# The sum of three weight quarters in the Mixer: two accumulating loads in place of an addition on VectorE, under a new list of instructions

## The chip, the cores and the metric

The kernel runs on one core of a Trainium2 chip. A core has five engines that run their own instruction streams: TensorE (PE in the profile, with its weight loads as PEld), VectorE (DVE), ScalarE (ACT), GpSimd (POOL) and SyncE (SP), and 16 DMA engines that serve the queues on which the engines put transfers. The metric is the device time in microseconds, and less is better. The kernel is launched once, and the weights lie in HBM in the layout that the kernel wants.

## The reference

One decoder layer on 512 tokens with 1,024 features, in float32:

```python
h = h + 0.5 * swiglu(rmsnorm(h, ffn1_norm), ffn1_w_gate, ffn1_w_up, ffn1_w_down)   # 1024 -> 2816 -> 1024
n = rmsnorm(h, mix_norm)
u, v, z, xbc, dt_raw = jnp.split(n @ w_in, IN_SPLITS, axis=-1)                     # u, v, z: 1024 columns each
ya = rmsnorm(chunked_spatial_gating(gelu(u), gelu(v), ...), gm_out_norm)
yb = mamba2_mixer(z, xbc, dt_raw, ...)                                             # conv, chunked SSD, silu(z), norm
h = h + jnp.concatenate([ya, yb], axis=-1) @ w_out
h = h + 0.5 * swiglu(rmsnorm(h, ffn2_norm), ffn2_w_gate, ffn2_w_up, ffn2_w_down)
gate = jax.nn.sigmoid(rmsnorm(h, ple_norm) @ ple_w_gate + ple_b_gate)
h = h + gate * (p @ ple_w_proj)
return rmsnorm(h, final_norm)
```

What matters here are the three products `n @ w_u`, `n @ w_v` and `n @ w_z` of the token mixer, each 512 x 1024 by 1024 x 1024.

## The kernel before, in words

**Precision.** Every float32 operand of a large product is split into a high part, the fp32r copy, and a low part, the rest. A product is three TensorE passes: high by high, high by low and low by high. For a weight tile of 128 x 1024 the split is a ScalarE copy into `whi` and a VectorE subtraction into `wlo` (`Parts.split`); the tile itself comes by one 512 KB load on SP's queue (`Parts.load`).

**Seven products.** The weights w_u, w_v and w_z are each cut into two blocks of 512 columns, and each block into four quarters of 512 rows by 256 columns: `src[0]`, `src[1]` are the upper and lower rows of the first 256 columns, `src[2]`, `src[3]` those of the second. A block is computed not by eight products of quarters but by seven products of sums of quarters, in the manner of Strassen and Winograd. The sums of the activations are made once. Those of the weights are made block by block, in `Quads.run`, most of them by the transfer itself: a load on GpSimd's queue with `accum_op=ALU.add` adds the quarter in HBM to the tile in SBUF. One product is 24 matmuls with 256 columns.

A block uses three tiles of weights: `w11` and `w22`, which live through most of the block and are changed and split again in between (pool `r4`, two buffers, shown as `r` in the profile), and `w`, which is used for one product (pool `raw`, three buffers). In the order of the program text: `w11` is loaded with `src[0]` and split for product 1; `w` gets `src[2] + src[0]` for product 7; `w22` is loaded with `src[3]`, split for later use, and `src[2]` is added to it by an accumulating load for the sum of products 5 and 6; product 4 uses its split of `src[3]`. Then VectorE adds `w22` to `w11`, so that `w11` is `src[0] + src[2] + src[3]`; that is split for product 6. `src[1]` is added to `w11` by an accumulating load, for product 3. Product 5 uses `w22`, product 2 a fresh `w` with `src[1]`. There are six such blocks: two each in `gates` (w_z), `values` (w_v, where weights and activations change sides on TensorE) and `outer` (w_u), called z0, z1, v0, v1, u0, u1 here.

**The order.** The program is not issued as it is written. Each call on an engine is recorded (`Recorder`), the records are grouped into units (a unit is one instruction, or a row of TensorE instructions with the same output), numbered from 0 in the order of the program text, and issued in the order of a list, `ORDER` (line 87), by `issue` under a manual schedule. There are 2,729 units. Each engine, and each queue of transfers, gets its instructions in the order of that list and runs them in that order; a semaphore wait is put in wherever an operand isn't ready or a buffer isn't free. Buffers are handed out in the order of the list too: a tile takes the first buffer that is free in its pool at its first use, and gives it back after its last. All instructions have line 1906 in the profile, since `issue` makes the call, so that they are told apart by the names of their tiles: `r` is w11 or w22, `raw` the tile `w`, `whi` and `wlo` the split, `xa` and `xb` the activations in the blocks of the Mixer, `xfa` and `xfb` in the SwiGLU stages, `m` and `u` the tiles of the SSD, `b` and `a` the accumulators in PSUM.

**Stages.** By the names of the tiles in the trace, the first SwiGLU runs to about 356 us, the Mixer's convolution part, SSD, blocks and `w_out` follow, the six blocks between 425 and 585 us interleaved with the SSD and the gating, then the second SwiGLU from about 680 us, the gated embedding, and the final norm (`factors`, `rows_out`) from about 1059 us: 32 transposes of 128 x 128 (`ident`), and sums of squares by matmuls with `ones`.

Of the kernel before, what the change touches and what calls it, by code (L numbers as in the profile page):

```python
# [27 lines left out]
ALU = mybir.AluOpType  # L28
# [48 lines left out]
for _name, _w in _VECS:  # L77
# [212 lines left out]
def layer_kernel(ctx: ExitStack, tc: tile.TileContext, a: dict, out: bass.AP):  # L290
# [1139 lines left out]
    class Quads:  # L1430
# [23 lines left out]
        def run(self, plain, summed):  # L1454
            src = self.src
            w11 = Parts("r4")
            w11.load(src[0])
            w11.split()
            ps_x, ps_a, ps_q = bank(), seeded(), bank()
            self.product(w11, 1, ps_x, True)  # L1460
            nc.scalar.copy(ps_a, ps_x)
# [552 lines left out]
```

## Time and profile before

| | |
|---|---|
| runs of the kernel before | 1073.25, 1074.03, 1074.38 us; median 1074.03 |
| the profiled execution | 1075.2 us |
| its span, first to last instruction | 1073.5 us |
| mean granted TensorE clock | 0.996 |
| data moved by DMA | 173.28 MB |

The profile is of one execution. Its own time is 1.7 us above its span, and 1.2 us above the median of the runs. Engine rows give busy time, share of the span and number of instructions. A row of a group names line, engine, operation, output `<-` inputs, shape and count, then the summed time with the mean in ns, then the idle time of that engine just before these instructions, with what ended most of it. A row of DMA issues gives the count, the KB of each and the median time from issue to landing. A row that begins with a time is an event, or a few in a row that are alike: start, duration, engine, what it did, `x` the count. A row of a stretch begins with its bounds, then its length and the busy time and number of instructions of PE, PEld, DVE, ACT and POOL, the granted clock, the mean busy share of the 16 DMA engines and GB/s. In the rows of the waits, the numbers are the idle time in us, how often, and the longest.

### The profile page before, as it was taken

The page shows a single profiled execution, that of the slowest core. Times are in us where ns is not written, and L with a number is a line of the kernel's source. Part 1 is how long each engine was busy: PE and PEld are TensorE (multiplying, and loading weights), DVE is VectorE, ACT ScalarE, POOL GpSimd, SP SyncE. Part 2 cuts the span into 40 slices and gives each one's busy share as a digit, 9 for nine tenths or more (in the row PEclk, how much of TensorE's full clock was granted, in tenths as well). Part 3 has the DMA queues.
Part 4 walks back from the last instruction along what each step waited for, and adds up shares of the span by engine and source line. Part 5 has one row for each costly group of instructions (what it writes and reads, how often), then busy time and mean ns, then how long its engine had stood idle before and what let it go on. Part 6 is the DMA issues. An engine that isn't in the chain of part 4 may idle for free.

```text
span 1073.5 us, 17640 instructions
## 1 busy us (share of the span) xinstructions
PE 1065.4 (99%) x7151; PEld 967.5 (90%) x7151; DVE 816.0 (76%) x1169; ACT 560.3 (52%) x781; POOL 77.1 (7%) x95
## 2 busy tenths in 40 slices
PE   9999999999999999999999999999999999999997
PEld 7899999999998878998999888999999999999887
DVE  6888676756577879999999667888766666757765
ACT  7555343444444537897766344655344343434544
POOL 1100000110100000000100000010100100000000
PEclk9999999999999999999999999999999999999998
DMA  9967775575633244776765444767936855734312
GB/s 322 250 169 204 202 191 197 146 209 137 177 79 99 62 135 131 182 216 164 204 144 127 135 136 106 213 187 198 261 98 197 232 142 145 186 121 112 112 53 79
DMA packets 52210, 173.28 MB, mean 161 GB/s; under 512 B 5920, under 2 KB 6176, under 8 KB 52128
## 3 DMA queue, kind: packets, MB, share of 16 engines
q1 hardware_dynamic: 34272, 117.98, 32.0%
q0 software_dynamic: 12256, 44.57, 23.1%
q10 hardware_dynamic: 5600, 9.60, 3.0%
q8 instruction: 56, 0.92, 0.3%
q14 instruction: 26, 0.21, 0.1%
HBM read 167.86 MB, written 4.26 MB: 160 GB/s over the span
## 4 chain that ended last, share of the span: by engine, by line
PE 99%; DMA 0%; ACT 0%; SPq 0%; DVE 0%; issue 0%; ACTq 0%
PE b L1906 81%; PE a L1906 18%; DMA g<-in_p 0%; SPq L1906 0%; DVE glo L1906 0%; ACT o L1906 0%; ACT ghi L1906 0%; ACT m L1906 0%; ACT b L1906 0%; ACTq L1906 0%
## 5 line engine op out<-in xcount | busy, mean ns | idle before, releaser
L1906 PE MATMUL b<-xfb,whi 128*128 128x256 f32 (+1 forms) x1704 | 298.1, 279 | 0.7 <-ACT b L1906 0.7
L1906 PEld LDWEIGHTS b<-xfb,whi 128*128 128x128 f32 x1704 | 260.8, 188 | 6.5 <-issue 1.0
L1906 PE MATMUL b<-xfb,wlo 128*128 128x256 f32 (+1 forms) x852 | 237.2, 278 | 0.0
L1906 ACT CAST whi<-raw 128x1024 fp32r<-128x1024 f32 (+1 forms) x131 | 136.4, 1042 | 148.5 <-PE b L1906 82.6
L1906 DVE TENSOR_TENSOR wlo<-raw,whi 128x1024 fp32r<-128x1024 f32 (+1 forms) x130 | 157.2, 1213 | 54.0 <-ACT whi L1906 51.4
L1906 PEld LDWEIGHTS b<-xfb,wlo 128*128 128x128 f32 x852 | 159.9, 188 | 0.5
L1906 PE MATMUL b<-xfa,whi 128*128 128x256 f32 (+1 forms) x696 | 124.2, 281 | 0.0
L1906 PEld LDWEIGHTS b<-xfa,whi 128*128 128x128 f32 x696 | 107.0, 188 | 2.9 <-DVE xfa L1906 0.5
L1906 PE MATMUL b<-xfa,wlo 128*128 128x256 f32 (+1 forms) x348 | 97.8, 281 | 0.0
L1906 ACT CAST whi<-rawb 128x1024 fp32r<-128x1024 f32 x51 | 53.5, 1050 | 67.1 <-PE b L1906 54.2
L1906 DVE TENSOR_TENSOR wlo<-rawb,whi 128x1024 fp32r<-128x1024 f32 x51 | 62.3, 1221 | 25.0 <-ACT whi L1906 25.0
L1906 ACT CAST whix<-rawd 128x1024 fp32r<-128x1024 f32 (+1 forms) x40 | 39.4, 986 | 76.0 <-PE a L1906 41.5
L1906 DVE TENSOR_TENSOR wlox<-rawd,whix 128x1024 fp32r<-128x1024 f32 (+1 forms) x40 | 45.7, 1142 | 34.0 <-ACT whix L1906 33.9
L1906 PE MATMUL b<-m,whi 128*128 128x512 f32 x224 | 69.5, 391 | 0.0
L1906 PEld LDWEIGHTS b<-xfa,wlo 128*128 128x128 f32 x348 | 65.4, 188 | 0.5
L1906 PE MATMUL b<-xb,whi 128*128 128x256 f32 (+1 forms) x280 | 61.9, 317 | 0.0
L1906 PE MATMUL b<-ghi,wlox 128*128 128x512 f32 x156 | 61.4, 394 | 0.0
L1906 PE MATMUL b<-glo,whix 128*128 128x512 f32 x156 | 61.2, 392 | 0.0
L1906 PE MATMUL b<-ghi,whix 128*128 128x512 f32 x156 | 60.7, 389 | 0.0
L1906 POOL DMA_DIRECT2D raw<-in_ffn_gu x32 | 31.7, 1034 | 344.2 <-DVE wlo L1906 126.3
L1906 PE MATMUL a<-ghi,wlox 128*128 128x512 f32 x140 | 55.2, 394 | 0.0
L1906 PE MATMUL a<-glo,whix 128*128 128x512 f32 x140 | 54.9, 392 | 0.0
(294 smaller groups left out, 2256.9 us busy)
## 6 DMA issues: line engine op xcount, KB each, us to landing
raw<-in_ffn_gu SPq DMA_DIRECT2D x57, 512.0 KB, 6.2
rawd<-in_ffn_down SPq DMA_DIRECT2D x40, 512.0 KB, 4.5
raw<-in_ffn_gu POOLq DMA_DIRECT2D x32, 512.0 KB, 7.6
rawb<-in_ffn_gu SPq DMA_DIRECT2D x31, 512.0 KB, 6.1
s<-in_ffn_gu SPq DMA_DIRECT2D x21, 512.0 KB, 4.9
s<-in_ffn_gu POOLq DMA_DIRECT2D x21, 512.0 KB, 7.9
raw<-in_w_out SPq DMA_DIRECT2D x16, 512.0 KB, 3.7
raw<-in_w_in SPq DMA_DIRECT2D x13, 512.0 KB, 3.8
```

The costliest lines, as they stand in the source:

```text
L1906: getattr(getattr(real, engine), what)(*(real_of(x) for x in args), **{k: real_of(x) for k, x in kw.items()})
```

## The change

In each of the six blocks the addition on VectorE goes. In its place `w11` gets two accumulating loads on GpSimd's queue: `src[2]` after the first split of `w11`, and `src[3]` later; each is 512 KB. Nothing that the block computes is different but for the order of that sum. `ORDER` is a new list for the whole program. With six instructions fewer and twelve more it has 2,735 units, and their numbers shift accordingly.

```diff
@@ -85,130 +85,130 @@
 ORDER = (
-    "1-2 5-7 9-10 13 12 11 0 3 14 16 18 24 20 15 17 19 25 21 26 41 27 29 42 38 37 40 39 43 8 34 32-33 35 "
...
@@ -1456,6 +1456,7 @@
             w11 = Parts("r4")
             w11.load(src[0])
             w11.split()
+            nc.gpsimd.dma_start(w11.raw, src[2], accum_op=ALU.add)
             ps_x, ps_a, ps_q = bank(), seeded(), bank()
             self.product(w11, 1, ps_x, True)
             nc.scalar.copy(ps_a, ps_x)
@@ -1463,6 +1464,7 @@
             w = Parts()
             w.load(src[2])
             nc.gpsimd.dma_start(w.raw, src[0], accum_op=ALU.add)
+            nc.gpsimd.dma_start(w11.raw, src[3], accum_op=ALU.add)
             w22 = Parts("r4")
             w22.load(src[3])
             w.split()
@@ -1474,7 +1476,6 @@
             nc.gpsimd.dma_start(w22.raw, src[2], accum_op=ALU.add)
             self.product(w22, 4, ps_q, False)
 
-            nc.vector.tensor_tensor(w11.raw, w11.raw, w22.raw, ALU.add)
             w11.split()
             nc.gpsimd.dma_start(w11.raw, src[1], accum_op=ALU.add)
             self.product(w11, 6, ps_a, False)
```

All lines of the list differ; it is left out here but for its first line before. What of it bears on the blocks: on GpSimd's queue, the new list has w11's load of `src[2]`, w11's of `src[3]` and then w22's of `src[2]` in the blocks z0, v0 and u1, and w22's load between w11's two in z1, v1 and u0; ScalarE makes w22's second split ahead of w11's in z0, z1 and u0. TensorE's instructions are the same by name and count, and 1,881 of 6,964 stand elsewhere in the order. In the final norm, four transposes stood ahead of the second half's sums of squares; in the new list all 32 stand behind them.

247 rows, old and new, of the table ORDER are left out of this document.

## The prediction

> **What bounds the kernel now.** I read the page first, then the waits of TensorE alone, then the Mixer stage (425 to 585 us) by windows.
>
> ```profile
> span 1073.5 us, 17640 instructions
> PE 1065.4 (99%) x7151; PEld 967.5 (90%) x7151; DVE 816.0 (76%) x1169; ACT 560.3 (52%) x781; POOL 77.1 (7%) x95
> ...
> DVE  6888676756577879999999667888766666757765
> ...
> q0 software_dynamic: 12256, 44.57, 23.1%
> ...
> PE 99%; DMA 0%; ACT 0%; SPq 0%; DVE 0%; issue 0%; ACTq 0%
> ```
>
> ```profile
> PE b L1906 <- DVE tmp L1906: 1.7, 1, 1.7
> PE b L1906 <- ACT b L1906: 0.7, 1, 0.7
> PE a L1906 <- ACT m L1906: 0.3, 1, 0.3
> ```
>
> ```profile
> core 0: us, PE busy (x) PEld busy (x) DVE busy (x) ACT busy (x) POOL busy (x), PEclk, DMA share, GB/s
> 425.00:585.00 160.00, 159.74 (x1334) 151.85 (x1333) 153.76 (x257) 126.12 (x217) 16.23 (x19) 1.00 0.70 175
> ```
>
> The chain that ended last is TensorE for 99% of the span. TensorE waits for another engine three times, 2.7 us in all; 1.7 of that is the wait for the first operand at the start, where the edit reaches nothing. In the Mixer, where the edit lies, TensorE is busy 159.74 of 160 us and VectorE 153.76, which is 96% (the nines of its row on the page). So VectorE is nearly full there, but it is not waited for: the 0.3 us is an ACT copy. Work taken from VectorE gives time back only where TensorE stood still for it, and these rows show no such place.
>
> The addition and its neighbours, in the first of the six blocks:
>
> ```profile
> 440.56 1.05 ACT L1906 CAST whi<-r 128x1024 fp32r<-128x1024 f32 x1 [0.75 <-DMA r<-in_w_z]
> 440.70 1.22 DVE L1906 TENSOR_TENSOR r<-r,r 128x1024 f32<-128x1024 f32 x1
> 442.34 1.05 ACT L1906 CAST whi<-r 128x1024 fp32r<-128x1024 f32 x1
> 443.42 1.23 DVE L1906 TENSOR_TENSOR wlo<-r,whi 128x1024 fp32r<-128x1024 f32 x1
> 444.94 0.80 PE L1906 MATMUL a<-xb,whi 128*128 128x256 f32 x2
> ```
>
> The addition starts when the load onto w22 has landed, the sum is split, and product 6 starts 0.3 us after the split's end at 444.65. The list in force is just in time there: TensorE had other work up to that moment.
>
> **What goes.** Six additions on VectorE:
>
> ```profile
> L1906 DVE TENSOR_TENSOR r<-r,r 128x1024 f32<-128x1024 f32 x6 | 7.3, 1224 | 0.7 <-DMA r<-in_w_u 0.7
> L1906 DVE TENSOR_TENSOR wlo<-r,whi 128x1024 fp32r<-128x1024 f32 x30 | 36.6, 1222 | 2.8 <-ACT whi L1906 2.7
> L1906 ACT CAST whi<-r 128x1024 fp32r<-128x1024 f32 x30 | 31.4, 1047 | 20.3 <-PE b L1906 7.7 <-DVE r L1906 3.6 <-PE a L1906 2.7
> ```
>
> 7.3 us of VectorE, all beside a busy TensorE: I take 0 for it. The bounds are 0 and the waits that TensorE has after the start, 0.7 + 0.3 = 1.0 us gained. Product 6 also no longer depends on w22's data, though in the new list ScalarE still has w22's second split ahead of w11's in three of the blocks (z0, z1, u0).
>
> **What comes.** Twelve accumulating loads of 512 KB on POOL's queue, two to a block. Their nearest rows are the accumulating loads that are there:
>
> ```profile
> q0 software_dynamic: 2448, 8.91, 33.3%
> ...
> r<-in_w_z POOLq DMA_DIRECT2D x4, 512.0 KB, 5.8
> ...
> r<-in_w_z SPq DMA_DIRECT2D x3, 512.0 KB, 3.7
> ...
> raw<-in_w_v POOLq DMA_DIRECT2D x2, 512.0 KB, 9.0
> raw<-in_w_u POOLq DMA_DIRECT2D x2, 512.0 KB, 7.7
> ```
>
> ```profile
> L1906 POOL DMA_DIRECT2D r<-in_w_z x4: 872/874/875, 434.5 to 474.1; - x4
> ```
>
> Issuing costs POOL 0.87 us each, 10 us on a queue that is busy 16 of 160 us: nothing on TensorE's path. The data: q0's 8.91 MB in this stage are 17 loads and take 33.3% of the 16 DMA engines, so 1.96 points each; twelve more are 23.5 points, and the stage's DMA share goes from 0.70 to about 0.94. The second load adds onto what the first wrote, so it waits in POOL's queue until that has landed. By the new list, what stands directly behind it is w22's own accumulating load in the blocks z0, v0 and u1; in z1, v1 and u0 w22's load goes between the two. Behind w22's load waits its second split, and behind that, on ScalarE, in z0 the split for product 6.
>
> The length of the new chain is the cost to look at. From the end of w11's first split to the finished sum are two landings, 2 x 5.8 = 11.6 us. Before, the addition could follow as soon as w22 had landed, 2.4 us after that split in the fourth block (520.38 to 522.76):
>
> ```profile
> 519.16 1.22 DVE L1906 TENSOR_TENSOR wlo<-r,whi 128x1024 fp32r<-128x1024 f32 x1
> ...
> 522.76 1.22 DVE L1906 TENSOR_TENSOR r<-r,r 128x1024 f32<-128x1024 f32 x1
> ```
>
> Such a block has to load w11 some 9 us earlier than it did. There are two r4 buffers, so the question is whether the pair turns over in time. With 2.27 us for a split (1.05 + 1.22), w11 holds its buffer for 3.7 + 2.27 + 11.6 + 2.27 + 5.8 + 2.27 = 27.9 us and w22 for 3.7 + 2.27 + 5.8 + 2.27 = 14.0. Two buffers make that 21.0 us to a block, against (23.3 + 14.0) / 2 = 18.7 before, where w11 has 3.7 + 2.27 + 5.8 for w22's landing, 1.22 for the addition, then 2.27 + 5.8 + 2.27. A block lasts 160 / 6 = 26.7 us. The margin shrinks from 8.0 to 5.7 us and stays above zero, so I take 0; the upper bound is in the rivals. Three landings a block (six for two buffers) use up 5.7 us when each becomes 1.9 us longer.
>
> One rule speaks against moving work from VectorE to these loads. POOL's issue took 872 to 875 ns four times out of four, in a stage where VectorE is busy 96%. The Trainium skill, "SBUF — State Buffer", section "SBUF: two separate sides", says that while VectorE holds the port pair which it shares with GpSimd, GpSimd cannot write the descriptors of its DMAs, and the load looks stalled. By that rule each of a block's two new loads could wait out one 1.22 us operation and the margin of 5.7 would be some 4.5; by the row nothing is held up. I go by the row.
>
> **The list.** It holds the same TensorE instructions before and after (I compared them by name), in another order, so TensorE's sum can change only through its pace. That is not constant:
>
> ```profile
> 509.00:516.00 7.00, 7.00 (x62) 7.00 (x61) 5.84 (x9) 6.17 (x8) 0.00 (x0) 1.00 0.87 300
> ...
> 519.00:526.00 7.00, 7.00 (x64) 7.00 (x64) 6.50 (x10) 5.97 (x12) 0.00 (x0) 1.00 0.99 219
> ```
>
> ```profile
> 507.51 0.94 PE L1906 MATMUL b<-m,m 128*128 128x128 f32 x6
> 508.20 0.36 PE L1906 MATMUL a<-whi,xa 128*128 128x256 f32 x1
> ...
> 517.23 1.20 PE L1906 MATMUL b<-u,m 128*64 128x128 f32 x13
> 518.37 0.38 PE L1906 MATMUL b<-whi,xb 128*128 128x256 f32 x1
> ```
>
> ```profile
> 48.50:61.00 12.50, 12.50 (x112) 12.50 (x112) 11.34 (x15) 10.31 (x14) 0.16 (x1) 1.00 0.51 116
> 707.50:720.00 12.50, 12.50 (x108) 12.50 (x107) 11.19 (x14) 8.36 (x10) 0.00 (x0) 1.00 0.41 100
> ```
>
> The four windows hold only matmuls of 256 columns at full clock, and TensorE never stops; still one pace is 12.5 us / 110.5 = 113.1 ns and the other 12.5 / 106.5 = 117.4 (1.5 taken off each count for the edges). A run keeps the pace with which it starts, until a matmul of another kind comes. The six blocks have 6 x 7 x 24 = 1,008 such matmuls; if about half are slow now (an estimate from the windows above, one each), all slow costs 2.2 us more and all fast 2.2 us less. The slow stretch at 509 follows the SSD matmuls `b<-m,m`, the fast one at 519 follows `b<-u,m`; the new list puts its longest Mixer run, 144 matmuls, behind those. I take -0.5, a little over a hundred matmuls at 4.3 ns.
>
> At the end the list moves four transposes. Now they stand ahead of the second half's sums; in the new list all 32 come after them.
>
> ```profile
> 1059.33 0.63 PE L1906 MATMUL b<-ident,h 128*128 128x128 f32 x4
> ...
> 1059.80 0.50 PE L1906 MATMUL b<-ones,ssum 128*128 128x1 f32 x4
> 1060.17 2.08 PE L1906 MATMUL b<-ones,sq 128*128 128x1 f32 x12
> ...
> 1062.11 5.97 PE L1906 MATMUL b<-ident,h 128*128 128x128 f32 x28
> ```
>
> 28 take 5.97 us, 0.213 each, so four more cost 0.85 at most; the sums start 0.47 earlier (1059.33 instead of 1059.80), and ScalarE scales the last half tile two operations earlier. Between 0 and +0.85 I take +0.3.
>
> **The sum**, on the profiled execution's own 1075.2 us (span 1073.5 and 1.7 around it): 0 for the additions, 0 for the loads, -0.5 and +0.3 for the list, so 1075.0. That execution is 1.2 above the median of the runs, 1074.03: forecast **1073.8**, its own range 1072 to 1076. A difference below 0.2%, 2.1 us, is about what can't be told from no change.
>
> **The rivals.**
>
> *Slower: the loads don't keep up.* Place: w11's buffer in the Mixer. For it: the share of 0.94, and rows in the same stage where an accumulating load takes 7.7 and 9.0 us instead of 5.8; the list is just in time (0.3 us above), so a late sum stops TensorE at once. Against: TensorE lost nothing at a share of 0.99 around 519. It decides from 1.9 us a landing. At 2.6 (between 7.7 and 9.0) a block loses 3 x (2.6 - 1.9) = 2.1 us; in the three blocks where w22's load is queued behind the second, that is 6 us with little given back: 1079 to 1080, less if only one or two blocks slip, 1076 to 1078. The Trainium skill, "DMA: Bandwidth & Descriptors", section "Rules for kernel authors", demands that wait for the earlier load's semaphore, so it can't be queued away.
>
> *Faster: the relief is used.* With 7.3 us free on VectorE, the new order could run all blocks at the quick pace and lose the waits of 0.7 and 0.3: -2.2 - 1.0 = -3.2, so 1070.8. For it: VectorE was full. Against: TensorE, the bound, has nothing left to give but pace, which the free time does not set.
>
> *The search undoes it.* The whole list is new, the two SwiGLU stages too, where nothing of the program changed. One product that comes late by one transfer in each of them, like the wait behind ACT of 0.7, and a slow pace in the blocks (2.2) make +3: 1077. For it: nothing but the number of moved instructions.
>
> **How the numbers follow.** Forecast 0.50, slower 0.20, faster 0.20, the undoing search 0.10. Faster by over 0.2%: the faster rival and a little of the forecast's edge, 0.23. Slower: the two others less what stays within the bound, 0.27. Within: 0.50. The range 1071.2 to 1078.8 leaves out the deep end of each side rival.
>
> **What would show it.** Right: VectorE 7 us lower, q0 at about 50.9 MB instead of 44.6, POOL with twelve more issues, TensorE's waits in the Mixer still near zero, its busy time within 2 us. Wrong: ACT or PE rows waiting for `DMA r<-in_w_*` in the Mixer and TensorE idle before `a<-xb,whi` (slower); TensorE's 1,008 matmuls quicker by 2 us (faster); idle time in the SwiGLU stages (the search).

## The result, and the profile after

The changed kernel takes 1080.71 us (median of four, 1079.80 to 1082.08) against 1073.64 of the kernel before; the ratio is 1.0069, 95% interval 1.0051 to 1.0086. It is slower, by less than 1% but clear of the noise. Two later series beside the kernel before, on two chips, gave 1.0040 (1.0027 to 1.0054) and 1.0044 (1.0030 to 1.0058).

The page of the kernel after:

```profile
span 1078.0 us, 17649 instructions
PE 1065.6 (99%) x7151; PEld 967.5 (90%) x7151; DVE 813.0 (75%) x1163; ACT 560.3 (52%) x782; POOL 85.5 (8%) x107
...
q0 software_dynamic: 13984, 50.86, 26.1%
...
PE 95%; DMA 2%; ACT 1%; DVE 1%; issue 0%; SPq 0%; ACTq 0%
```

The edit is there as it was read: six VectorE instructions fewer, twelve more on POOL, and q0 moves 50.86 MB instead of 44.57. TensorE is as busy as before (1065.4). New is the last line: 5% of the chain is no longer TensorE, where it was 1%. The waits of TensorE in the kernel after:

```profile
PE b L1907 <- DVE tmp L1907: 2.2, 2, 1.7
PE b L1907 <- ACT a L1907: 1.8, 1, 1.8
PE b L1907 <- ACT b L1907: 0.7, 1, 0.7
PE a L1907 <- DVE wlo L1907: 0.6, 2, 0.3
PE b L1907 <- DVE wlo L1907: 0.6, 1, 0.6
PE a L1907 <- ACT m L1907: 0.3, 1, 0.3
PE b L1907 <- DVE glo L1907: 0.2, 1, 0.2
```

The old ones (1.7, 0.7, 0.3) are all there still. Of the new ones, 0.2 us is near the start, at 7.9 us; the other five lie between the first matmul of the blocks and the first of the second SwiGLU. That stretch before, and then after:

```profile
430.24:676.05 245.81, 245.55 (x1719) 222.99 (x1718) 214.03 (x350) 159.86 (x261) 18.00 (x21) 1.00 0.61 158
```

```profile
430.27:681.53 251.26, 247.46 (x1720) 224.40 (x1719) 210.47 (x346) 159.23 (x260) 26.12 (x31) 1.00 0.70 171
```

It is 5.45 us longer: TensorE stands still 3.80 us of it instead of 0.26, and is busy 1.91 us longer for the same matmuls. Up to 430 us the two traces agree within 0.03 us; the second SwiGLU and the embedding take 381.6 and 381.7 us. The final norm takes 15.85 us before (from 1057.63) and 14.81 after (from 1063.23), which is the clock's doing, see the last section. 0.03 + 5.45 + 0.12 - 1.04 is the 4.56 us between the spans.

The stop of 1.8 us is in the first block, z0. By time, in the kernel after:

```profile
427.60 0.85 POOL L1907 DMA_DIRECT2D r<-in_w_z  x1 [5.10 <-DMA r<-in_w_z]
...
428.31 0.33 SPq L1907 DMA_DIRECT2D raw<-in_w_z  x1
...
437.61 1.04 ACT L1907 CAST whi<-raw 128x1024 fp32r<-128x1024 f32 x1 [3.16 <-DMA raw<-in_w_z]
...
439.28 0.57 ACT L1907 COPY a<-b 128x512 f32<-128x512 f32 x1
...
439.90 0.50 PE L1907 MATMUL b<-xb,whi 128*128 128x256 f32 x2 [1.75 <-ACT a L1907]
```

```profile
428.31 9.20 DMA raw<-in_w_z
```

The second new load onto w11 is issued at 427.60, as soon as the first has landed. 0.71 us later SP issues a plain load, the quarter for product 2. It lands after 9.20 us; the plain loads of `raw` in the blocks had medians of 5.6 to 6.1 before. ScalarE waits 3.16 us for it, behind that instruction stands the copy of product 1's sum, and product 2 must not overwrite that bank until it is copied. What is late here is not w11's sum but a load that has nothing to do with it. The stop of 0.30 us ahead of z0's product 6, at 446.88, follows from it: w11's sum had landed at 437.28, but its split stands on ScalarE behind w22's and behind the work that the late load had held up.

The other three stops are in u0, the fifth block. VectorE there, and then TensorE:

```profile
550.75 1.17 DVE L1907 TENSOR_TENSOR wlo<-raw,whi 128x1024 fp32r<-128x1024 f32 x1
...
554.60 0.68 DVE L1907 TENSOR_TENSOR tmp<-ident,rtok 128x512 f32<-128x512 f32 x1
```

```profile
551.98 0.38 PE L1907 MATMUL b<-xb,wlo 128*128 128x256 f32 x1 [0.59 <-DVE wlo L1907]
...
555.34 1.13 PE L1907 MATMUL b<-tmp,ones 128*128 128x512 f32 x2 [0.58 <-DVE tmp L1907]
...
557.01 0.38 PE L1907 MATMUL a<-xb,wlo 128*128 128x256 f32 x1 [0.31 <-DVE wlo L1907]
```

The first two wait for a split and for a small tile of the gating, which stand on VectorE behind the statistics of the gating's norm. Only the third, 0.31 us, waits for w11's sum.

### The profile page after: what moved, and what is told of

It is laid out like the page before. It is cut to its first block, busy times and chain, and to the rows that moved or that the text cites. A ratio compares the mean times of both kernels' runs of the same rounds, so it can differ in the third digit from the quotient of the medians.

```text
span 1078.0 us, 17649 instructions
## 1 busy us (share of the span) xinstructions
PE 1065.6 (99%) x7151; PEld 967.5 (90%) x7151; DVE 813.0 (75%) x1163; ACT 560.3 (52%) x782; POOL 85.5 (8%) x107
## 3 DMA queue, kind: packets, MB, share of 16 engines
q0 software_dynamic: 13984, 50.86, 26.1%
## 4 chain that ended last, share of the span: by engine, by line
PE 95%; DMA 2%; ACT 1%; DVE 1%; issue 0%; SPq 0%; ACTq 0%
PE b L1907 78%; PE a L1907 17%; DMA r<-in_w_u 1%; DMA raw<-in_w_z 1%; DVE wlo L1907 0%; DMA g<-in_p 0%; ACT whi L1907 0%; ACT m L1907 0%; ACT xa L1907 0%; ACT o L1907 0%; ACT u L1907 0%; SPq L1907 0%; DVE glo L1907 0%; ACT ghi L1907 0%; DVE ssum L1907 0%
```

## The experiments

Ratios are to the kernel before in the same series of runs. "Stretch" is the one above, from the first matmul of the blocks to the second SwiGLU, in the profiled execution (245.81 before, 251.26 changed).

| kernel | median us | ratio (95%) | stretch |
|---|---|---|---|
| old block, new list | 1088.16 | 1.0133 (1.0118 to 1.0148) | 260.2 |
| new list, no loads | 1078.17 | 1.0034 (1.0022 to 1.0046) | 248.60 |
| new block, old list | 1102.16 | 1.0259 (1.0243 to 1.0275) | 273.9 |
| first load only | 1076.40 | 1.0026 (1.0017 to 1.0035) | 248.19 |
| changed, second series | 1078.69 | 1.0040 (1.0027 to 1.0054) | 250.35 |
| both loads small | 1076.16 | 1.0024 (1.0014 to 1.0033) | 248.19 |
| old tail | 1077.21 | 1.0032 (1.0020 to 1.0044) | 249.35 |
| five moves | 1081.82 | 1.0070 (1.0057 to 1.0083) | 254.1 |
| changed, third series | 1079.36 | 1.0044 (1.0030 to 1.0058) | 249.78 |
| two loads changed over | 1077.94 | 1.0033 (1.0021 to 1.0044) | 247.96 |
| changed over, two moves | 1077.41 | 1.0036 (1.0023 to 1.0048) | 249.15 |
| first load small | 1077.54 | 1.0027 (1.0016 to 1.0038) | 249.39 |

The span goes with the mean granted clock (last section), so that spans are best compared at one clock. At 0.995, over all series, it is 1073.1 to 1074.6 us before (seven executions), 1075.8 to 1076.1 with the new list and no loads or small ones (five), and 1077.0 to 1080.4 changed (seven). So the list costs something, and the loads cost something on top.

**The old block under the new list.**

```diff
-            nc.gpsimd.dma_start(w11.raw, src[2], accum_op=ALU.add)
...
-            nc.gpsimd.dma_start(w11.raw, src[3], accum_op=ALU.add)
...
+            nc.vector.tensor_tensor(w11.raw, w11.raw, w22.raw, ALU.add)
```

> The new list with the old block: the twelve loads are out, and the addition on VectorE stands right ahead of w11's second copy. Two theories. Theory loads: TensorE's new stops (1.8 us at 439.9, and 0.6 + 0.6 + 0.3 us from 552 to 557) come from the landings of the new loads, and the list only decides where they show; then this runs within 0.15% of the kernel before, 1073 to 1075.5, and TensorE waits less than 1.0 us between 412 and 680 us. Theory list: the new order has put products ahead of their data whatever w11's sum is made by; then the stops at 440 and 552 to 557 stay, and it runs at 1079 to 1081.

Neither came: 1088. TensorE's waits:

```profile
PE b L1905 <- DVE wlo L1905: 5.2, 1, 5.2
PE a L1905 <- DVE wlo L1905: 3.0, 4, 1.3
```

The addition waits for w22's landing with VectorE's queue behind it; in u0 the split of the tile for product 2 stands there and is 5.2 us late. The new list leaves no place for the addition, so this run doesn't tell the theories apart.

**The new list without the loads**, both lines out.

> The changed kernel without the twelve new loads, list and all else the same; it leaves out adding the two quarters to w11, so that products 6 and 3 use another sum. Theory loads: 1073 to 1075.5, no TensorE stop over 0.3 us between 412 and 660 us, and the plain load of raw<-in_w_z that took 9.2 us at 428.3 takes 5 to 7. Theory list: 1079 to 1081, with the stops where they are.

It lies between the two. The stop at 440 is gone. Of the waits that the kernel before doesn't have, 0.6 behind `tmp` and 0.6 behind `wlo` are those of u0; the third is at 6.3 us, far ahead of the Mixer:

```profile
PE b L1904 <- DVE tmp L1904: 2.2, 2, 1.7
...
PE b L1904 <- DVE wlo L1904: 0.6, 1, 0.6
PE b L1904 <- ACT whi L1904: 0.4, 1, 0.4
```

```profile
430.08:678.68 248.60, 247.16 (x1721) 224.41 (x1719) 210.04 (x346) 159.32 (x260) 17.57 (x21) 1.00 0.57 149
```

With neither additions nor loads the new list loses 2.8 us against the kernel before: 1.2 more of standing still, 1.6 more of TensorE's busy time. The first theory falls as a whole account: the list costs by itself. The rest, 251.26 - 248.60 = 2.7 in this trace and 1.8 and 1.2 in the two later ones of the changed kernel, comes with the loads.

**The new block under the old list**: w11's loads behind its first split and behind w22's accumulating load, the addition out.

> The new block under the old list: w11's first new load right after its first split, the second right behind w22's accumulating load, the addition gone. Theory loads: the old list has the sum 1.2 us after w22's landing and product 6 some 4 us behind it; now a landing of 5.7 to 7 us stands there, so that each of six blocks is 2 to 6 us late: 1086 to 1110. Theory list: the loads are covered: 1072 to 1076.

1102, as the theory of the loads had it, though the lateness sits in three long stops and not in each of six blocks. The waits, and the stretch:

```profile
PE a L1906 <- ACT whi L1906: 7.8, 1, 7.8
PE b L1906 <- ACT a L1906: 6.6, 1, 6.6
PE a L1906 <- ACT a L1906: 4.4, 1, 4.4
```

```profile
430.50:704.41 273.91, 253.41 (x1719) 229.60 (x1717) 207.83 (x344) 159.89 (x261) 27.78 (x32) 0.96 0.64 162
```

The loads are far from free in that order. Of the 28.1 us that the stretch is longer, 20.2 are standing still; the other 7.9 are TensorE's busy time, at a granted clock of 0.96 instead of 1.00 (last section). The new list, for all it costs, wins back 21 to 24 of the 28 us.

**Only the first load.**

> The changed kernel with only the first of each block's two loads (src[2]); it leaves out adding src[3] to w11. Theory loads, as a chain of two landings and as traffic by the second load at 427.6 (landed after 9.68 us) beside the plain load that TensorE then waited for: both are gone, 1073 to 1076, and raw<-in_w_z at 428.3 lands in 5 to 7 us. If already the first load costs: 1076 to 1079. Theory list: 1079 to 1081.

The stretch is no longer than without loads, 248.19. The time, 1076.40, is 0.4 us above the range for no cost, but the kernel without loads isn't quicker, so the first load shows no price. One extra landing fits in; the cost comes with the second.

**Both loads cut to 64 of 1,024 columns, and only the first so cut.**

```diff
-            nc.gpsimd.dma_start(w11.raw, src[2], accum_op=ALU.add)
+            nc.gpsimd.dma_start(w11.raw[:, :64], src[2][:, :64], accum_op=ALU.add)
```

> The changed kernel with its twelve new loads cut to 64 of 1,024 columns: same issues on GpSimd's queue, same waits, 32 KB instead of 512; it leaves out the rest of the two sums. If the bytes of the loads cost (landings of 7 to 10 us beside each other): as without the loads, 1075 to 1078, raw<-in_w_z of 428.3 landing in 5 to 7 us. If the two waits in a row and the queue cost, whatever is moved: 1079 to 1082.

> The changed kernel with the first of the two loads cut to 64 columns, the second whole; it leaves out the rest of src[2] in w11's sum. The chain of two landings is then some 3.5 us shorter, while the second load still moves its 512 KB. If the chain's length costs: 1075 to 1077.5, as without loads. If the second load's bytes cost beside other loads: 1077.5 to 1081.

With both small, all issues and waits are there and nothing is lost against the kernel without loads (248.19 in the stretch): GpSimd's queue and the waits as such cost nothing. What costs hangs on the bytes, either through longer landings in the chain or through traffic beside other loads. With the second whole, the stretch is 249.39, although the chain is short; but its time, 1.0027, can be told neither from that of the small ones nor from the changed kernel's 1.0044 in the same series, so the share of each stays open.

**The changed kernel twice more.**

> The changed kernel itself beside the three that are derived from it. At equal granted clock its span stood 6.5 us above that of the kernel before (1078.0 at 0.998 against 1071.5; 1080.2 at 0.995 against 1073.6). The same again: 1079.5 to 1082.

> The changed kernel again, since its two series stood 7.1 and 4.8 us over the kernel before, and the load of raw<-in_w_z took 9.2 us in the trace of the one and 5.3 in that of the other. If that load's landing is what differs: a median of 1078 to 1082, and a trace with a long landing shows the stop of 1.8 us near 440, one with a short landing doesn't.

The second series, 1078.69, came out below the 1079.5 to 1082 expected; the third is in its range. The landing of the load that stopped z0, and the stretch, in the second series and then in the third:

```profile
DMA to landing us min/median/max: 5.3/5.3/5.3
...
429.96:680.31 250.35, 247.53 (x1721) 224.33 (x1720) 209.91 (x346) 159.40 (x260) 26.34 (x32) 1.00 0.71 171
```

```profile
DMA to landing us min/median/max: 8.6/8.6/8.6
...
429.94:679.72 249.78, 246.92 (x1720) 224.05 (x1719) 209.40 (x346) 159.33 (x260) 26.12 (x31) 1.00 0.69 172
```

With 5.3 us there is no stop near 440, with 8.6 one of 1.1, with 9.2 one of 1.8. The first load had landed after 7.7 us in the second series, so that the second went out at 429.33, behind the plain load at 428.00; in the first series it had landed after 5.7, and the second went out ahead. An earlier landing of the first load made the later stop. What the one execution saves there it loses elsewhere in part: in the second series TensorE waits 0.95 us in z0's product 6. w11's sum isn't late there either, it had landed at 436.85. Late is w22's accumulating load (issued at 433.90, landed after 8.1 us), and ScalarE splits w22 ahead of w11:

```profile
442.01 1.99 ACT L1907 CAST whi<-r 128x1024 fp32r<-128x1024 f32 x2 [2.08 <-DMA r<-in_w_z]
```

**The two loads of z0 and z1 changed over.** In the new list SP loads the quarter for product 2 of z1 (unit 1245) ahead of that of z0 (1057), though z0's is used some 39 us earlier; z0's load then has to wait for a buffer of `raw`:

```diff
-1245 1034 1057
+1057 1034 1245
```

> The changed kernel with two loads on SP's queue changed over: by the new list the quarter for z1's product 2 is loaded near 420 and the one for z0's product 2 only near 428, though z0 uses it first. With z0's at 420 it lands near 425, ahead of the new loads. If the stop of 1.8 us at 440 comes from that load beside the accumulating one: it is gone, and the time is 1 to 2.5 us below the changed kernel of the same call, or the same if that has no such stop. If w11's sum is what is late in z0: a stop of 0.5 to 1.5 us stays at product 6, near 444 to 447.

The stop is gone although the load at 428 is as slow as ever; it is z1's now, and nobody needs it soon:

```profile
DMA to landing us min/median/max: 8.1/8.1/8.1
...
429.82:677.78 247.96, 246.60 (x1720) 224.03 (x1719) 208.89 (x346) 159.26 (x260) 26.11 (x31) 1.00 0.71 173
```

With all twelve loads in it this stretch is as short as that without any. In the changed kernel's three traces z0 has most of the standing still that came with the loads: 1.75 and 0.30 us in the first, 0.2 and 0.95 in the second, 1.1 and 0.3 in the third; here it has none. In time the gain stays unproved: 1.0033 and the changed kernel's 1.0044 in the same series have intervals that overlap.

**Two moves in u0 on top of that**: the split of the tile for product 2 (unit 1573) and the tile from rtok (1386) ahead of the statistics.

```diff
-1378 1492 ... 1495 1573 1498 ... 1385 1496-1497 1566 1499-1500 1386
+1378 1573 1492 ... 1495 1498 ... 1385-1386 1496-1497 1566 1499-1500
```

> The swap, and in u0 the split of the tile for product 2 and the making of the rtok tile ahead of the statistics behind which they stood, which took both stops near 550 and 554 away before. If these three places and the landings are all that stands between the kernels beside pace and restarts: 1.1 us below the swap alone, 1075 to 1077.5, still 1 to 3 above the kernel before. If the loads cost wherever they stand: 1077.5 to 1081.

Both stops are gone, and others of the same size came, at product 6:

```profile
PE a L1906 <- ACT whi L1906: 0.9, 1, 0.9
PE a L1906 <- DVE wlo L1906: 0.8, 1, 0.8
```

Once TensorE no longer loses 1.1 us ahead of it, product 6 comes up at 552.42, when w11's sum has only just landed (552.09) and isn't split. Two stops that follow each other cover one another; only the longer chain is paid. 1077.41 is in the first range, but 0.5 us below the swap alone instead of 1.1, and the intervals overlap.

**Five moves**: the old tail, the two of u0, w11's second load behind w22's in z0, and w11's ahead of w22's in u0, with their splits changed over.

> The old tail, and five moves in two of the blocks. In z0 w11's load of src[3] goes behind w22's accumulating load, so that it doesn't run beside the load that TensorE waited for. In u0 w11's two loads go ahead of w22's, and the second splits of w11 and w22 change places; the split of the tile for product 2, and the making of the rtok tile, go ahead of the statistics behind which they stood. If the stops read in the trace are the cause and each is a matter of place: 1.8 + 0.5 us at z0 and 1.5 us at u0 and 0.6 in the tail are gone, 1075 to 1077.5. If the loads need the DMA engines wherever they stand, new stops come up elsewhere: 1078 to 1081.

1081.82 lies above both ranges. New stops came, as the second case had it, in both places where w11's load was put elsewhere:

```profile
444.95 0.50 PE L1907 MATMUL a<-xb,whi 128*128 128x256 f32 x2 [0.96 <-ACT whi L1907]
...
555.06 0.50 PE L1907 MATMUL a<-xb,whi 128*128 128x256 f32 x2 [1.17 <-ACT whi L1907]
```

**The old tail.**

> The changed kernel with the last 222 units in the old list's order, so four of the 32 transposes stand ahead of the second half's sums again. If the tail of the new list costs what the spans leave over beside the Mixer (6.5 less 5.5): 0.5 to 1.0 us below the changed kernel at equal clock. If that remainder is the clock's: no difference over 0.3.

Final norm with the new order (first load only) and with the old one, both at full clock:

```profile
1059.49 0.50 PE L1905 MATMUL b<-ones,ssum 128*128 128x1 f32 x4
...
1062.98 3.69 PE L1905 MATMUL b<-ident,h 128*128 128x128 f32 x32
```

```profile
1060.91 0.50 PE L1907 MATMUL b<-ones,ssum 128*128 128x1 f32 x4
...
1064.80 3.25 PE L1907 MATMUL b<-ident,h 128*128 128x128 f32 x28
```

From the first sum to the end of the span (1072.7 and 1074.1) are 13.2 us in each. The tail costs nothing; the 1.0032 against 1.0040 in that series is no difference.

## Why the prediction was wrong

The forecast was no change at 1073.8; measured is +7.1 in the first series and about +5 in the other two. The slower rival gave 1079 to 1080 and was held at 0.20; its time came, its mechanism only in part.

*The additions at 0*: right as far as the runs go. No run takes the additions alone out of the old list; but without them and without the loads nothing is faster, and none of the waits of 0.7 and 0.3 went. The relief of VectorE was worth nothing. Its busy time fell by 3.0 us, not 7: the durations of its instructions add up to 7.8 less, but they overlap less.

*The loads at 0*: the step that failed. It set two buffers against a block's length and found 5.7 us to spare. None of the stops read above came from those two buffers. The margin that counts is the list's, and the prediction had its size in the first row of the block, 0.3 us, and used it only inside the rival. It also named z0's chain, in which w11's split waits on ScalarE behind w22's landing, and put no price on it; in the second series that chain cost 0.95 us. Landings grew much less than the 1.9 us from which that rival was to decide:

```profile
r<-in_w_z POOLq DMA_DIRECT2D x8, 512.0 KB, 6.7
r<-in_w_v POOLq DMA_DIRECT2D x8, 512.0 KB, 6.3
r<-in_w_u POOLq DMA_DIRECT2D x8, 512.0 KB, 5.9
```

5.8, 5.5 and 6.0 before. The sum also left out the transfers that stand beside the new ones: the costliest stop came from a plain load which the edit doesn't touch. "TensorE lost nothing at a share of 0.99" was read from one window of 7 us; the stage's share came to 0.87, not 0.94, and TensorE lost time all the same. And the list was searched for the three blocks in which w22's load stands behind w11's second; its SP queue, in which z1's quarter goes ahead of z0's, was not.

*The list through its pace alone*: a second step that failed. The new order has stops of its own, the two of u0, 1.2 us with neither additions nor loads.

*The pace at -0.5*: wrong sign. By the starts of the matmuls, some 410 of the 1,008 ran at the slow pace before and some 530 after, 120 x 4.3 ns = +0.5 us. One slow run after:

```profile
503.00:510.00 7.00, 7.00 (x62) 7.00 (x61) 5.92 (x10) 6.55 (x15) 0.12 (x1) 1.00 0.94 217
```

The whole of TensorE's busy time in the stretch grew by 1.9; the other 1.4 wasn't foreseen, and its cause stays open.

*The tail at +0.3*: nothing. The 0.213 us a transpose was measured while the clock stood at 0.5; at full clock it is 3.25 / 28 = 0.116.

*GpSimd's port*: the row was the right one to go by. With VectorE busy 145.25 of the stage's 160 us the issues took

```profile
L1907 POOL DMA_DIRECT2D r<-in_w_z x8: 844/860/861, 421.6 to 475.2; - x8
```

against 872 to 875 before, and the kernel with small loads, which has every issue, lost nothing. What the Trainium skill says in "SBUF — State Buffer", section "SBUF: two separate sides", that GpSimd's descriptors wait while VectorE holds the shared port, shows in no row here. The prediction also read it too widely: the section says this of VectorE's 2-port modes, and that `tensor_tensor`, which is most of VectorE's work in the Mixer, has no such mode. The wait for the earlier load's semaphore, which the Trainium skill demands in "DMA: Bandwidth & Descriptors", section "Rules for kernel authors", does show. In the chain of the kernel after, w11's two loads in u0:

```profile
541.87 5.66 DMA r<-in_w_u
547.52 0.28 issue
547.81 6.75 DMA r<-in_w_u
```

The second goes out 0.28 us after the first has landed, and the pair takes 12.7 us, where the prediction had 11.6.

*The search that undoes it* was held at 0.10 and placed in the SwiGLU stages, "one product that comes late by one transfer". That is z0's stop word for word, and two of u0's stops are the new list's alone, but all of them sit in the Mixer; the second SwiGLU with the embedding takes only 0.12 us more. The rival's price was also added up short: a wait of 0.7 in each of two stages and a pace of 2.2 make 3.6, not 3.

What stays open: the executions of one changed kernel at one granted clock spread over 2 to 3 us of span (in the third series at 0.997: 1075.6 to 1078.3 changed, 1075.2 to 1076.9 with the loads changed over; at 0.995: 1077.0 and 1078.8, and 1075.9 to 1079.0), those of the kernel before over less (0.997: 1072.2 to 1072.8; 0.995: 1073.9 and 1074.6). The stops read above are those of one execution each, and for the kernel with the loads changed over it was the quickest of the four at that clock. That landings differ from one execution to the next, as the traces show for one load, would explain such a spread; that it is the whole of it isn't shown. None of the kernels run here beats the kernel before.

## What to carry to other kernels

Where a bound engine never waits because its order is just in time, the room for a new transfer is what stands ahead of the next instruction that needs it, row by row, and not a sum over a stage or a buffer's life. Price a new transfer also by the transfers of other queues that will be in the air with it, and look in those queues for one that is loaded in the wrong order: two numbers changed over in the list took the largest stop away. A new order is a change of its own: run it without the rest of the edit and read its waits. Work taken from an engine that nobody waited for gave nothing here, however full it was.

## What was not expected of the hardware

**A plain load beside an accumulating one.** In all twelve traces with the new list SP issues a plain load of 512 KB at 428 us. It took 5.0 and 5.3 us when the accumulating load was issued 1.0 and 1.3 us behind it, and 7.9 to 9.2 in the four traces where that was issued between 0.7 ahead and 0.4 behind. With no whole accumulating load within 3 us it took 4.9 to 6.4. The accumulating load itself landed after 8.1 to 9.7 us in those four; the medians of such loads before were 5.5 to 6.0.

**A long stop takes the clock with it.** In the new block under the old list the granted clock is at 0.5 for 6.8, 10.2 and 6.8 us, each time from within one of the three stops of 4.4, 7.8 and 6.6 us. The stop of 5.2 us in the old block under the new list has 6.8 us of it, and the stops in u0 with five moves (1.17 and 0.76 us, 0.5 apart) have 3.4 behind them. The other traces, with stops of up to 1.8 us, have none of it in the Mixer. So a stop can cost more than its own length.

**The clock at the end.** The granted clock falls to 0.5 in the final norm, at another time in each trace, for 3.4 or 6.8 us, and in two of them only behind the last matmul. In the trace of before it is 6.8 us, and the 28 transposes take 5.97 us; in the changed kernel's it is 3.4 us:

```profile
1066.72 5.36 PE L1907 MATMUL b<-ident,h 128*128 128x128 f32 x32
```

Over 17 executions of the kernel before in one series the span goes with the mean granted clock, 1070.5 to 1071.0 us at 0.999 and 1073.1 to 1074.1 at 0.995. Two profiles of kernels that differ by less than 1% should be set side by side at equal clock, or stage by stage, as the 4.5 us between the spans here, which are 5.6 up to the final norm, show.
